# The row of mean squares in a two-mixer decoder layer: squares move under standing ones, and the row travels through DRAM ahead of its power

## The chip, the cores and the metric

The kernel runs on one core of one Trainium2 chip. The metric is the device time of one execution in microseconds (us), the median of several runs. One execution was also recorded by the profiler; its engines are TensorE (PE, with the weight loads as PEld), VectorE (DVE), ScalarE (ACT), GpSimd (POOL) and the queue of DMA issues on SyncE (SP). A second queue of DMA issues belongs to ScalarE.

## The reference

One layer on 1024 tokens of width 1024. The input is normed and modulated, one wide projection gives the parts, a gated spatial mixer gives `y_a`, and a state-space mixer (SSD) with 32 heads in 8 groups, in chunks of 128 tokens, gives `y_b`. What matters here is the step between the SSD mixer and its projection: an RMS norm over the 256 channels of each group, for each token.

```python
y_b = ssd_scan(xh, dt, a, bm, cm) + xh * d_skip[:, None]
yz = (y_b.reshape(b, s, SSM_D_INNER) * silu(ssm_z)).reshape(b, s, SSM_GROUPS, SSM_D_INNER // SSM_GROUPS)
y_b = rms_norm(yz, ssm_norm_w.reshape(SSM_GROUPS, -1)).reshape(b, s, SSM_D_INNER)
merged = sigmoid(g_a) * (y_a @ w_proj_a) + sigmoid(g_b) * (y_b @ w_proj_b)
return x + gate[:, None, :] * (merged @ w_out)
```
So for each group and token the kernel needs `(mean(yz*yz) + eps) ** -0.5`, a row of 1024 numbers per group.

## The kernel before

Channels lie on the 128 partitions and tokens along the free axis. Large products are made by a seven-product scheme on halves, in split precision. The order of the work is written out by hand for TensorE and for SyncE's loads: `mm`, `tp` and `load` (lines 80 to 90) are kept in program order. `store` (line 92) issues a DMA from ScalarE's queue and is placed by a scheduler, as are most operations of VectorE, ScalarE and GpSimd; those inside `tc.high_priority()` go first. The scheduler works with a simulated time of its own.

**The mixer phase** (about 932 to 1157 us) runs 32 steps, two groups taking turns, four steps of 256 tokens for each group. A step has three items, each a *slot*: `front` (the products inside the chunk `yi` and the new state `sp`), `back` (the product with the state `yn`, then `evacuate`) and `prep` for a later step (transposes and products into `pc` and `px`, then VectorE's products `dcy` on line 1027 and `xd`, `xe` on line 1023). Between the items TensorE is fed matmuls of the first projection (`pma`, drawn by `draw`). `later(n, f)` runs `f` n slots on. `fetch` loads the tiles `sl` and `dcy` of a step; there are five sets, so a load waits for the step five back to be done with its set.

**The row.** `evacuate` (line 1074) writes `yz`, the gated output, into a tile of 2 x 512 columns, of which there are four; the last operation is on GpSimd (line 1089). Eight steps later the same place is written again. After every second step `post` (line 1091) stores `yz` to `yb_d`, and
- 5 slots later `squares` (line 1106) squares it in place on ScalarE and adds the two halves on GpSimd (line 1109);
- 17 slots later `post2` (line 1111) sums the squares over the partitions: for each of four blocks of 128 tokens, the block of squares is the standing operand and a column of ones moves, which gives one column of `pq`. VectorE scales it into `ssq` (line 1117), tokens on partitions. When both halves of a group are there, GpSimd raises the 8 columns to the power −0.5 (line 1121);
- 8 slots after that `post3` (line 1125) transposes the 8 columns on TensorE into 8 rows of 128, VectorE copies them (line 1131) into a constant tile that is no longer used, and a store writes them to `rs_d`.

Groups 6 and 7 end last. Their second halves are squared into two tiles `sq` of their own, taken from two rings of two slots (line 1101), and summed in the next stage.

**The last stage** begins with the second projection: seven products `p1, p5, p2, p3, p6, p7, p4` of eight units each (`units`, line 1418). Unit `u` multiplies, then `ahead(u)` (line 1570) issues the loads of unit `u+6` and makes the operands of unit `u+4`. `y_load` (line 1406) loads a piece of `yb_d` (tile `yn`) and, for every second piece, the row of `rs_d` spread over the partitions (tile `rb`); `y_norm` (line 1414) multiplies them. The rows of groups 0 to 3 are wanted first, those of 6 and 7 from the loads of unit 20 on. `post2` of groups 6 and 7 stands behind units 1 and 4, `post3` behind units 4 and 6 (lines 1606 to 1613).

Of the kernel before, what the change touches and what calls it, by code (L numbers as in the profile page):

```python
# [12 lines left out]
ALU = mybir.AluOpType  # L13
# [3 lines left out]
P = 128  # L17
D = 1024
S = 1024
KT = D // P  # L20
NCH = S // P
NG = 8
# [3 lines left out]
EPS = 1e-6  # L26
# [9 lines left out]
def hybrid_kernel(  # L36
# [7 lines left out]
    V, A, G, PE = nc.vector, nc.scalar, nc.gpsimd, nc.tensor  # L44
# [8 lines left out]
    def dt_(shape, name):  # L53
        return dram.tile(shape, F32, name=name, tag=name)

    acs_d = dt_([NG, 4, HPG, 256], "acs_d")
    rs_d = [dt_([1, S], f"rs_d{g}") for g in range(NG)]
    v_d = dt_([NG, P, NCH * P], "v_d")
    ya_d = [dt_([P, S], f"ya_d{g}") for g in range(NG)]
    mt_d = [dt_([P, S], f"mt_d{g}") for g in range(NG)]  # L60
# [9 lines left out]
    def cst(shape, name, dt=F32):  # L70
        return const.tile(shape, dt, name=name, tag=name)
# [6 lines left out]
    pin = tc.keep_in_program_order  # L78

    def mm(acc, l, r, first=True, last=True):  # L80
        pin(PE.matmul(acc, l, r, start=first, stop=last))  # L81

    def tp(dst, src, idn):
        pin(PE.transpose(dst, src, idn))  # L84
# [4 lines left out]
    def load(dst, src):  # L89
        pin(nc.sync.dma_start(dst, src))  # L90

    def store(dst, src):
        nc.scalar.dma_start(dst, src)

    ident = cst([P, P], "ident")
    make_identity(nc, ident)
    ones = cst([P, P], "ones")
    G.memset(ones, 1.0)
    tri = cst([P, P], "tri")
    G.affine_select(out=tri, in_=ones, compare_op=ALU.is_ge, fill=0.0, base=0,  # L100
                    pattern=[[1, P]], channel_multiplier=-1)
    nhalf = cst([P, NCH], "nhalf")
# [13 lines left out]
    cwt = cst([P, P], "cwt")  # L116
# [9 lines left out]
    ssq = cst([P, NG * NCH + 24], "ssq")  # L126
# [365 lines left out]
    def later(delay, f, *a):  # L492
        tasks.append((slot[0] + delay, f, a))
# [478 lines left out]
    class Group:  # L972
# [118 lines left out]
        def post(self, q):  # L1091

            g = self.g
            for j in range(2):
                store(yb_d[2 * g + j][:, q * 512 : (q + 1) * 512], self.yz[q][:, j])
            yz = self.yz[q]
            if g < NG - 2 or q == 0:
                later(5, self.squares, yz, [yz[:, j] for j in range(2)])
                later(17, self.post2, q, [yz[:, 0]])
            else:  # L1100
                self.late = [turn(r, f"sq{g}", F32) for r in (y1_r, ym_r)]
                with tc.high_priority():
                    for j in range(2):
                        A.activation(self.late[j], yz[:, j], AF.Square)
# [4 lines left out]
            G.tensor_add(sq[0], sq[0], sq[1])  # L1109

        def post2(self, q, sq):
            g = self.g
            pq = rows_bank[0](f"pq{g}_{q}")
            for i in range(4):
                for j, t in enumerate(sq):
                    mm(pq[:, i : i + 1], t[:, i * P : (i + 1) * P], ones[:, 0:1], j == 0, j == len(sq) - 1)
            V.tensor_scalar(ssq[:, g * NCH + q * 4 : g * NCH + q * 4 + 4], pq[:, 0:4], 1.0 / 256, EPS,  # L1117
                            op0=ALU.mult, op1=ALU.add)
            if q == 1:
                c8 = slice(g * NCH, (g + 1) * NCH)  # L1120
                G.tensor_tensor(ssq[:, c8], ssq[:, c8], nhalf, op=ALU.pow)
                if g < NG - 2:
                    later(8, self.post3)

        def post3(self):

            g = self.g
            pr = rows_bank[0](f"pr{g}")
            tp(pr[0:NCH, 0:P], ssq[:, g * NCH : (g + 1) * NCH], ident)
            row = (cwt, tri)[g % 2][0:NCH, :]  # L1130
            V.tensor_copy(row, pr[0:NCH, 0:P])
            store(rs_d[g].rearrange("o (c p) -> (o c) p", p=P), row)

    groups = [Group(g) for g in range(NG)]
    rows_bank = [bank]
# [42 lines left out]
    def turn(r, name, dt=F32R):  # L1178
        tags, at = r
        at[0] += 1  # L1180
        return take(name, tags[(at[0] - 1) % len(tags)], dt)
# [187 lines left out]
    def banks(name, c):  # L1369
        return [psb.tile([P, 512], F32, name=f"{name}{j}", tag=f"b{c}{j}") for j in range(4)]  # L1370
# [12 lines left out]
    def slot_tile(name, dt=F32):  # L1383
        tag = room.pop(0)
        t = hp.tile([P, 512], dt, name=name, tag=tag)
        tags_of[name] = tag
        return t
# [82 lines left out]
    def multiply(u, ps):  # L1470
        nm, k = units[u]
        first = nm in ("p1", "p5", "p2", "p3")
        a, (bh, bl) = aops.pop(u), bops.pop(u)
        for j in range(4):
            js = slice(j * P, (j + 1) * P)
            for n, (v, r) in enumerate(((0, bh), (0, bl), (1, bh))):
                pin(PE.matmul(ps[j], a[:, v, js], r, start=first and n + k == 0, stop=n == 2 and k == KT - 1,  # L1477
                              skip_group_check=not first))
# [3 lines left out]
    def gate_load(b, h):  # L1482
        hs = slice(h * 512, (h + 1) * 512)
        th, ma = gate_slot(f"tg{b}_{h}"), gate_slot(f"ma{b}_{h}")
        load(th, th_d[(KT + b) * P : (KT + b + 1) * P, hs])
        load(ma, mt_d[b][:, hs])
        gates[b, h] = th, ma
# [82 lines left out]
    def ahead(u):  # L1570
        if u + LOAD < len(units):
            loads(u + LOAD)
        if u + LEAD < len(units):
            operands(u + LEAD)
# [15 lines left out]
    BESIDE = [(j // 2, wo_load, ("b11", j)) for j in range(4)] + [(2 + j, wo_load, ("t1", j)) for j in range(4)]  # L1590
    BESIDE += [(2 + j, wo_split, ("b11", j)) for j in range(4)]
    BESIDE += [(3 + j, row_load, (j,)) for j in range(5)] + [(j + 4, split, ("s1", j - 1)) for j in (1, 3)]
    for u, (nm, k) in enumerate(units):
        if k == 0:
            if nm == "p1":
                psy = banks("yp5", "y")
                psx = banks("x", "x")
                rows_bank[0] = lambda name: psy[("pr6", "pr7", "pq6_1", "pq7_1").index(name)]
            elif nm in ("p2", "p3"):
                psy = banks(f"y{nm}", "y")  # L1600
            elif nm == "p6":
                room.extend(rb_r[0])
            ps = psy if nm in ("p2", "p5", "p3") else psx
        multiply(u, ps)
        ahead(u)
        if nm == "p1" and k in (1, 4):
            late = groups[NG - 2 + k // 4]
            late.post2(1, late.late)
        if nm == "p1" and k == 4:
            for tags, _ in (y1_r, ym_r):  # L1610
                room.extend(tags)
        if nm == "p1" and k in (4, 6):
            groups[NG - 4 + k // 2].post3()
        if k % 2 and nm in GATES:
            gate_load(GATES[nm][0] + k // 2, GATES[nm][1])
        if nm == "p4":
            for at, f, a in BESIDE:
                if at == k:
                    f(*a)
        if k % 2 and more and nm not in ("p2", "p5"):  # L1620
            merged(*more.pop(0))
        if k == KT - 1:
            for j in range(4):
                with tc.high_priority():
                    if nm == "p1":
                        t = slot_tile(f"c11_{j}")
                        A.copy(t, psx[j])
                        more.append((j, 0, t, f"c11_{j}"))
                    elif nm == "p2":
                        V.tensor_add(more[j][2], more[j][2], psy[j])  # L1630
                    elif nm == "p5":
                        t = slot_tile(f"p5_{j}")
                        A.copy(t, psy[j])
                        sums.append(t)
                    elif nm == "p3":
                        t = slot_tile(f"p3_{j}")
                        V.tensor_add(t, sums[j], psy[j])
                        sums.append(t)
                    elif nm == "p6":
                        V.tensor_add(sums[4 + j], sums[4 + j], psx[j])  # L1640
                        more.append((j, 1, sums[4 + j], f"p3_{j}"))
                    elif nm == "p7":
                        V.tensor_add(sums[j], sums[j], psx[j])
                        more.append((4 + j, 1, sums[j], f"p5_{j}"))
                    elif nm == "p4":
                        merged(4 + j, 0, None, None)
# [166 lines left out]
```

## Time and profile before

| What | us or share |
|---|---|
| median of 3 runs | 1408.84 (1404.32 to 1409.13) |
| the profiled execution, own time | 1407.67 |
| its span in the profile | 1405.9 |
| granted TensorE clock | 0.997 |
| chain that ended last: TensorE, DMA, VectorE, GpSimd | 80%, 8%, 5%, 2% |
| DMA moved | 283.37 MB, mean 202 GB/s |

Start times in the rows are microseconds from the start of the span. A row of a timeline has the start, the time it takes, engine, line, operation, what is written from what, and how many were merged; in square brackets stands how long the engine was idle before it and what ended that. A row of the chain of work has a start, a length and what was at work. A row by tile has the shortest, middle and longest duration in nanoseconds, and the first and last start. Matmuls overlap in TensorE's pipeline, so the distance of two starts says more than a duration.

### The profile page before, as it was taken

The page shows a single profiled execution, that of the slowest core. Times are in us where ns is not written, and L with a number is a line of the kernel's source. Part 1 is how long each engine was busy: PE and PEld are TensorE (multiplying, and loading weights), DVE is VectorE, ACT ScalarE, POOL GpSimd, SP SyncE. Part 2 cuts the span into 40 slices and gives each one's busy share as a digit, 9 for nine tenths or more (in the row PEclk, how much of TensorE's full clock was granted, in tenths as well). Part 3 has the DMA queues.
Part 4 walks back from the last instruction along what each step waited for, and adds up shares of the span by engine and source line. Part 5 has one row for each costly group of instructions (what it writes and reads, how often), then busy time and mean ns, then how long its engine had stood idle before and what let it go on. Part 6 is the DMA issues. An engine that isn't in the chain of part 4 may idle for free.

```text
span 1405.9 us, 20633 instructions
## 1 busy us (share of the span) xinstructions
PE 1377.1 (98%) x7035; PEld 1139.9 (81%) x7035; DVE 1062.4 (76%) x1863; ACT 797.0 (57%) x1471; POOL 213.0 (15%) x208
## 2 busy tenths in 40 slices
PE   8999999999999999999999999999999999999997
PEld 6688888888888888888887888888888877878886
DVE  4786776777778889889788796388667767876976
ACT  5764576556656665556565555677766723322443
POOL 0000000000000011111000010038778740000001
PEclk9999999999999999999999999999999999999999
DMA  8653343343344777787675774598778749878903
GB/s 263 173 165 98 113 120 105 105 121 120 116 125 134 214 202 239 236 248 232 192 221 156 240 214 135 173 353 318 262 253 296 275 168 328 320 231 296 350 33 120
DMA packets 273150, 283.37 MB, mean 202 GB/s; under 512 B 15341, under 2 KB 223637, under 8 KB 273045
## 3 DMA queue, kind: packets, MB, share of 16 engines
q1 hardware_dynamic: 185684, 198.52, 44.4%
q10 hardware_dynamic: 87360, 83.54, 17.8%
q8 instruction: 55, 0.90, 0.3%
q14 instruction: 51, 0.41, 0.1%
HBM read 194.55 MB, written 87.46 MB: 201 GB/s over the span
## 4 chain that ended last, share of the span: by engine, by line
PE 80%; DMA 8%; DVE 5%; POOL 2%; issue 2%; ACT 1%; SPq 1%; ACTq 0%; DVEq 0%; POOLq 0%
PE xcb L574 6%; PE xuz L574 6%; PE xz L574 6%; PE xx L574 5%; PE xg L574 5%; PE x L1477 4%; PE yp L1477 4%; PE ox L1676 3%; PE yuz L574 3%; PE ycb L574 3%; PE pma L81 3%; PE xv L574 3%; PE yz L574 3%; PE yg L574 3%; PE yx L574 3%; DMA dcy<-acs_d 3%
## 5 line engine op out<-in xcount | busy, mean ns | idle before, releaser
L793 POOL TENSOR_TENSOR wog<-wog,gb 128x256 f32<-128x256 f32 x16 | 18.3, 1159 | 676.6 <-PE zz L574 413.3
L1007 ACT ACTIVATE dcy<-dcy,nacs 128x128 f32<-128x128 f32 x256 | 78.6, 388 | 14.9 <-POOL dcy L1002 14.5
L1002 POOL TENSOR_SCALAR_AFFINE_SELECT dcy<-dcy 128x1024 f32<-128x1024 f32 x32 | 35.0, 1095 | 135.7 <-ACT ea L999 132.3
L999 ACT ACTIVATE ea<-dcy 64x512 f32<-64x512 f32 x64 | 40.1, 626 | 14.2 <-DMA dcy<-acs_d 13.8
L920 ACT ACTIVATE ac<-ac 128x1024 f32<-128x1024 f32 x32 | 33.9, 1060 | 23.0 <-DVE ac L918 22.8
L81 PE MATMUL pma<-yh,wah 128*128 128x512 f32 x128 | 43.3, 419 | 0.0
L1027 DVE TENSOR_TENSOR dcy<-dcy,pc 128x1024 f32<-128x1024 f32 x32 | 39.0, 1218 | 4.8 <-PE pc L84 3.0
L81 PE MATMUL pma<-yh,wal 128*128 128x512 f32 x128 | 42.5, 413 | 0.0
L1089 POOL TENSOR_TENSOR yz<-y,sl 128x512 f32<-128x512 f32 x32 | 41.4, 1295 | 1.1
L1087 DVE TENSOR_TENSOR ym<-yn,ea 128x512 f32<-128x512 f32 (+1 forms) x32 | 19.9, 622 | 28.5 <-PE yn L81 28.3
L81 PE MATMUL pma<-yl,wah 128*128 128x512 f32 x128 | 40.1, 394 | 0.0
L1088 POOL TENSOR_TENSOR y<-y,ym 128x512 f32<-128x512 f32 (+1 forms) x32 | 36.6, 1144 | 14.4 <-DVE ym L1087 14.4
L81 PEld LDWEIGHTS yn<-sl,st 128*128 128x128 f32 x224 | 30.3, 190 | 8.3 <-issue 4.4
L81 PE MATMUL yn<-sl,st 128*128 128x128 f32 x224 | 31.6, 276 | 4.9 <-DVE st L1057 4.9
L1416 DVE SCALAR_TENSOR_TENSOR yn<-yn,par,rb 128x512 f32<-128x512 f32 x32 | 24.0, 749 | 15.7 <-DMA yn<-yb_d 15.5
L81 PE MATMUL sp<-xe,bn 128*128 128x256 f32 x112 | 32.6, 408 | 3.3 <-DVE ssq L1117 1.7
L81 PE MATMUL yi<-dcy,xd 128*64 128x128 f32 x512 | 35.7, 283 | 0.0
L918 DVE SCALAR_TENSOR_TENSOR ac<-c2x,cwt,ac 128x1023 f32<-128x1023 f32 (+2 forms) x24 | 31.2, 1300 | 5.3 <-ACT ac L916 5.1
L918 DVE SCALAR_TENSOR_TENSOR ac<-c2cb,cwt,ac 128x1023 f32<-128x1023 f32 (+2 forms) x24 | 31.1, 1296 | 4.4 <-ACT ac L916 4.3
L1691 POOL TENSOR_TENSOR r<-r,fnw 128x512 f32<-128x512 f32 x2 | 2.5, 1296 | 203.7 <-DMA out_dram<-r 203.7
L1055 POOL TENSOR_TENSOR st<-st,cd 128x256 f32<-128x256 f32 x48 | 32.1, 668 | 8.0 <-PE yn L81 5.3
L918 DVE SCALAR_TENSOR_TENSOR ac<-c1cb,cwt,ac 128x1023 f32<-128x1023 f32 (+2 forms) x24 | 31.6, 1318 | 1.3 <-ACT ac L916 1.3
(2980 smaller groups left out, 4390.9 us busy)
## 6 DMA issues: line engine op xcount, KB each, us to landing
sl<-s_d SPq DMA_DIRECT2D x32, 768.0 KB
s_d<-ac ACTq DMA_DIRECT2D x32, 512.0 KB
dcy<-acs_d SPq DMA_DIRECT2D x32, 512.0 KB
aw<-in_ada_w_dram SPq DMA_DIRECT2D x16, 512.0 KB
wbr<-in_w_proj_b_dram SPq DMA_DIRECT2D x64, 128.0 KB
wb_d<-wbb ACTq DMA_DIRECT2D x32, 256.0 KB
wb_d<-wbc ACTq DMA_DIRECT2D x32, 256.0 KB
yb_d<-yz ACTq DMA_DIRECT2D x32, 256.0 KB
```

The lines of the kernel that those rows point to most:

```text
L81: pin(PE.matmul(acc, l, r, start=first, stop=last))
L574: pin(PE.matmul(ps, lw[:, k * P : (k + 1) * P], r[k], start=first and n + k == 0, stop=n == 2 and k == 3, skip_group_check=not first))
L918: V.scalar_tensor_tensor(ac[:, s:], cc[:, : S - s], conv_wt[:, 3 - s, i : i + 1], ac[:, s:], op0=ALU.mult, op1=ALU.add)
L920: A.activation(ac, ac, AF.Silu)
L999: A.activation(ea[hh * HD : (hh + 1) * HD], dcy.rearrange("p (j e) i l -> p e j (i l)", e=2)[hh * HD : (hh + 1) * HD, hh], AF.Exp)
L1002: G.affine_select(out=d8, in_=d8, compare_op=ALU.is_ge, fill=-1e30, base=0, pattern=[[0, 2 * HPG], [1, P]], channel_multiplier=-1)
L1007: A.activation(dcy[:, h, i, :], dcy[:, h, i, :], AF.Exp, bias=sub[:, i, h : h + 1])
L1027: V.tensor_tensor(d3, d3, pc[:, 0:256].unsqueeze(1).to_broadcast([P, HPG, 256]), op=ALU.mult)
L1088: G.tensor_add(y1[:, :, t0:], y1[:, :, t0:], m[:, :, t0:])
L1089: G.tensor_mul(yz, y1, sl[:, 4:6])
L1477: pin(PE.matmul(ps[j], a[:, v, js], r, start=first and n + k == 0, stop=n == 2 and k == KT - 1, skip_group_check=not first))
L1676: pin(PE.matmul(ps, a[:, tsl], b[:, cs], start=first and n + j == 0, stop=n == 2 and j == 3, skip_group_check=not first))
```

## The change

`post2` comes 13 slots behind `post` instead of 17. The ones stand now (128 x 32) and a block of 128 squares moves; each of the four blocks goes into a strip of 32 partitions of one PSUM tile, every row of a strip holding the same sums. VectorE scales all 128 x 128 of it into the first 128 columns of the squares' own tile, and a store writes one row of each strip, four rows of 128, to a new DRAM row `ms_d`. `post3` is now a load from `ms_d` back into `ssq`, eight neighbouring tokens to a partition; `post4`, six slots on, is the power on GpSimd, now kept in program order; `post5`, three slots on, stores the result to `rs_d`. The transpose and its PSUM bank, the copy and the two constant tiles it was written to drop out. In the last stage the three steps stand behind units 3, 5 and 6 for group 6, and 7, 9 and 10 for group 7; `post2` stays behind units 1 and 4.

```diff
-                later(17, self.post2, q, [yz[:, 0]])
+                later(13, self.post2, q, [yz[:, 0]])
...
             pq = rows_bank[0](f"pq{g}_{q}")
-            for i in range(4):
-                for j, t in enumerate(sq):
-                    mm(pq[:, i : i + 1], t[:, i * P : (i + 1) * P], ones[:, 0:1], j == 0, j == len(sq) - 1)
-            V.tensor_scalar(ssq[:, g * NCH + q * 4 : g * NCH + q * 4 + 4], pq[:, 0:4], 1.0 / 256, EPS,
-                            op0=ALU.mult, op1=ALU.add)
-            if q == 1:
-                c8 = slice(g * NCH, (g + 1) * NCH)
-                G.tensor_tensor(ssq[:, c8], ssq[:, c8], nhalf, op=ALU.pow)
-                if g < NG - 2:
-                    later(8, self.post3)
+            for j, t in enumerate(sq):
+                for i in range(4):
+                    mm(pq[32 * i : 32 * i + 32, 0:P], ones[:, 0:32], t[:, i * P : (i + 1) * P], j == 0, j == len(sq) - 1)
+            row = sq[0][:, 0:P]
+            V.tensor_scalar(row, pq[:, 0:P], 1.0 / 256, EPS, op0=ALU.mult, op1=ALU.add)
+            store(ms_d[g][:, q * 512 : (q + 1) * 512].rearrange("o (i p) -> (o i) p", p=P), row[0:P:32, :])
+            if q == 1 and g < NG - 2:
+                for n, f in ((8, self.post3), (14, self.post4), (17, self.post5)):
+                    later(n, f)
 
         def post3(self):
 
-            g = self.g
-            pr = rows_bank[0](f"pr{g}")
-            tp(pr[0:NCH, 0:P], ssq[:, g * NCH : (g + 1) * NCH], ident)
-            row = (cwt, tri)[g % 2][0:NCH, :]
-            V.tensor_copy(row, pr[0:NCH, 0:P])
-            store(rs_d[g].rearrange("o (c p) -> (o c) p", p=P), row)
+            load(ssq[:, self.g * NCH : (self.g + 1) * NCH], ms_d[self.g].rearrange("o (p c) -> (o p) c", p=P))
+
+        def post4(self):
+
+            c8 = ssq[:, self.g * NCH : (self.g + 1) * NCH]
+            pin(G.tensor_tensor(c8, c8, nhalf, op=ALU.pow))
+
+        def post5(self):
+
+            store(rs_d[self.g].rearrange("o (p c) -> (o p) c", p=P), ssq[:, self.g * NCH : (self.g + 1) * NCH])
...
+    late_todo = {3: groups[NG - 2].post3, 5: groups[NG - 2].post4, 6: groups[NG - 2].post5,
+                 7: groups[NG - 1].post3, 9: groups[NG - 1].post4, 10: groups[NG - 1].post5}
...
-        if nm == "p1" and k in (4, 6):
-            groups[NG - 4 + k // 2].post3()
+        late_todo.get(u, lambda: None)()
```

More of the change, by code (lines that the diff above doesn't have):

```diff
@@ L57, in hybrid_kernel @@
     rs_d = [dt_([1, S], f"rs_d{g}") for g in range(NG)]
+    ms_d = [dt_([1, S], f"ms_d{g}") for g in range(NG)]
     v_d = dt_([NG, P, NCH * P], "v_d")
@@ L1597, in hybrid_kernel @@
                 psx = banks("x", "x")
-                rows_bank[0] = lambda name: psy[("pr6", "pr7", "pq6_1", "pq7_1").index(name)]
+                rows_bank[0] = lambda name: psy[1 + ("pq6_1", "pq7_1").index(name)]
             elif nm in ("p2", "p3"):
```

## Prediction

> **What bounds the kernel now.** I read the page's first part, then the busy time by stretches of the mixer phase, then the chain of work.
>
> ```profile
> PE 1377.1 (98%) x7035; PEld 1139.9 (81%) x7035; DVE 1062.4 (76%) x1863; ACT 797.0 (57%) x1471; POOL 213.0 (15%) x208
> ```
> ```profile
> 940.00:980.00 40.00, 39.95 (x300) 34.24 (x299) 33.77 (x57) 27.20 (x73) 30.87 (x31) 1.00 0.90 310
> 1100.00:1130.00 30.00, 27.75 (x207) 24.20 (x208) 21.65 (x42) 18.88 (x49) 23.49 (x25) 1.00 0.64 219
> 1160.00:1200.00 40.00, 37.77 (x183) 31.50 (x184) 30.99 (x51) 16.03 (x29) 3.29 (x2) 1.00 0.93 336
> ```
> Over the span TensorE is busy 98%, so a microsecond of TensorE work counts nearly everywhere. The stretches (columns: TensorE, weight load, VectorE, ScalarE, GpSimd, clock, DMA share) say that the phase of the change is less simple: at 940 DMA is 0.90 busy and GpSimd 31 of 40 us, at 1100 GpSimd has 23.5 of 30, and at 1160 DMA is at 0.93. The chain shows what ends last in each:
>
> ```profile
> 960.66 6.55 DMA dcy<-acs_d
> 988.51 1.05 PE pq L81 x8
> 1040.04 0.79 PE pq L81 x8
> 1046.30 0.79 PE pq L81 x8
> 1065.33 0.79 PE pq L81 x8
> 1072.06 0.79 PE pq L81 x8
> 1122.14 1.60 POOL ssq L1121
> 1131.06 1.64 POOL ssq L1121
> 1133.31 2.27 DMA yn<-yb_d
> 1145.70 0.79 PE pq L81 x8
> 1181.51 1.66 POOL ssq L1121
> ```
> The chain changes owner: loads of dcy, then TensorE from about 1030 to 1079, then GpSimd to 1133, then loads of the last stage. So of 14 sums of squares (tile pq) only six stand on the chain, and of the eight powers (ssq, L1121) three. What is taken from the others buys idle time.
>
> **TensorE, part by part.** A sum has four matmuls, each recorded twice: squares standing, one column of ones moving. After, 32 columns of ones stand and 128 columns of squares move, into four strips of 32 partitions. The nearest rows in four strips are the matvec's (tile pm, first rows), with 256 moving columns:
>
> ```profile
> 981.06 0.95 PE L81 MATMUL pq<-ones,yz 128*128 128x1 f32 x8
> 981.94 1.09 PE L81 MATMUL yi<-dcy,xd 128*64 128x128 f32 x16
> 14.95 1.07 PE L81 MATMUL pm<-aw,scz 128*32 128x256 f32 x16
> ```
> ```profile
> 23.90 0.58 PEld L81 LDWEIGHTS pm<-aw,scz 128*32 128x32 f32 x15
> ```
> Before: 981.94 − 981.06 = 0.88 us for 8 records. After, from below: 15 loads of 32 columns in 0.58 us, 0.039 each, so 8 take 0.31. From above: 1.07/16 = 0.067 with twice the columns, so 0.54; if strips did not overlap at all, 0.88 as now. I take 0.40, near the lower end, because half the columns move; it saves **0.48 per sum**. The Trainium skill, TensorEngine Tiling (Array Packing), section Tiling Modes, speaks against it: changing the mode (not just the tile) drains TensorE, and here the array goes to four strips and back 16 times. It gives no figure; by an estimate from the two pm rows, a drain of 1.07 − 0.58 = 0.49 us would eat the saving. This hangs on that page: by that rule the third rival below results, and the trace is not against it, though the 1.07 holds its own mode changes.
>
> On the chain, six sums give 6 × 0.48 = **−2.9**. The transposes of post3 go, 0.11 each:
>
> ```profile
> 1138.78 0.11 PE pr L84
> ```
> Four of six in the phase lie in TensorE stretches: **−0.4**.
>
> **VectorE and ScalarE.** The eviction grows from 128x4 to 128x128; the copies of 8x128 go.
>
> ```profile
> L1117 DVE TENSOR_SCALAR ssq<-pq x14: 150/152/163, 983.4 to 1150.4; 128x4 f32<-128x4 f32 x14
> L1131 DVE COPY cwt<-pr x3: 269/269/269, 1031.8 to 1139.4; 8x128 f32<-8x128 f32 x3
> ```
> The copy also reads 128 columns from PSUM, so I take 0.27: 16 × 0.12 = 1.9 more, 8 × 0.27 = 2.2 less, nothing in sum. The place matters more. With 13 slots instead of 17 (three slots a step: front, back, prep) the sum falls between back and prep, not between prep and front. It pushes prep's pc matmuls back by 0.40 and the eviction pushes the product dcy (L1027) by up to 0.27; where VectorE's chain through prep leads, that is lost. I count four of the 14 such, and the 0.40 alone, since the eviction is at least not longer than the copies that went: 4 × 0.40 = **+1.6**; bounds 0 and 14 × 0.67 = 9.4.
> ScalarE issues 16 stores to ms_d more and 8 to rs_d as before, at 0.3 us in its sequencer. A store waiting for VectorE holds what stands behind it on ScalarE:
>
> ```profile
> 1181.98 1.14 ACT L1455 CAST p5bh<-yn 128x512 fp32r<-128x512 f32 x2 [6.60 <-DVE cwt L1131]
> ```
> That is the store of rs_d today: the cast behind it came 6.60 late. In the mixer phase I cost the new stores at nothing, since ScalarE is 27 of 40 us busy; without that cover it is 16 × 0.3 = 4.8.
>
> **GpSimd.** The pow keeps its 1.65 us but goes 14 slots behind the sums. For groups 4 and 5 that is behind the last step, when GpSimd is done: the two on the chain (1122, 1131) leave it. Those of groups 2 and 3 come in, at about 1091 and 1098, where GpSimd has gaps. From 0 to −3.2; I take one pow, **−1.6**. The mixer phase sums to −2.9 − 0.4 + 1.6 − 1.6 = **−3.3**.
>
> **Waits that tighten.** Sums need the squares' add on GpSimd; and the tile yz is now held until the ms_d store has landed.
>
> ```profile
> L1089 POOL TENSOR_TENSOR yz<-y,sl x32: 1271/1286/1608, 941.7 to 1146.0; 128x512 f32<-128x512 f32 x32
> 992.27 1.29 POOL L1109 TENSOR_TENSOR yz<-yz 128x512 f32<-128x512 f32 x1
> 1008.91 0.95 PE L81 MATMUL pq<-ones,yz 128*128 128x1 f32 x8
> 1046.14 0.95 PE L81 MATMUL pq<-ones,yz 128*128 128x1 f32 x8
> 1053.67 1.27 POOL L1089 TENSOR_TENSOR yz<-y,sl 128x512 f32<-128x512 f32 x1
> 1014.94 1.12 ACTq L93 DMA_DIRECT2D yb_d<-yz  x2
> 1022.37 0.63 ACT L1108 ACTIVATE yz<-yz 128x512 f32<-128x512 f32 x1 [2.95 <-DMA yb_d<-yz]
> ```
> A step is (1146.0 − 941.7)/31 = 6.6 us, so four slots are 8.8. The closest add ends at 993.56, 15.35 before its sum: 6.5 stay. The closest reuse comes 7.5 behind its sum (1053.67 − 1046.14); 16.3 stay for eviction, issue and a landing. Stores on this queue land in up to 1022.37 − 1014.94 = 7.4. Both hold, at no cost. Without the cover, a store landing later would delay yz, then the DMA issue behind it on SyncE that waits for yz's engine.
>
> **The last stage.** The sums of groups 6 and 7 (16 records each) and their transposes stand among the products:
>
> ```profile
> 1164.07 1.84 PE L81 MATMUL yp<-ones,sq 128*128 128x1 f32 x16
> 1165.77 0.49 PE L1477 MATMUL x<-p1bh,p1a 128*128 128x512 f32 x1
> 1183.21 0.27 PE L84 MATMUL yp<-ident,ssq 128*8 128x128 f32 x1 [1.69 <-POOL ssq L1121]
> ```
> Each sum goes from 1.70 to 0.80: −1.8. Two transposes: −0.2. TensorE's 1.69 of waiting for group 7's power goes, for no TensorE work needs it any more: −1.7. Together **−3.7**. What is late next is the operands of p5. In their way stands the new load of ms_d on SyncE's pinned queue: at unit 7 it stands behind p5's loads for k=5 and ahead of all others, and holds them until the store has landed.
>
> ```profile
> 1178.65 0.32 SPq L90 DMA_DIRECT2D rb<-rs_d  x1
> ```
> ```profile
> 1181.27 0.15 DVE L1117 TENSOR_SCALAR ssq<-yp 128x4 f32<-128x4 f32 x1
> 1186.56 0.75 DVE L1416 SCALAR_TENSOR_TENSOR yn<-yn,par,rb 128x512 f32<-128x512 f32 x1 [0.55 <-DMA yn<-yb_d]
> 1187.23 0.68 DVE L1456 TENSOR_TENSOR p5bl<-yn,p5bh 128x512 fp32r<-128x512 f32 x1
> ```
> ```profile
> 1186.09 0.39 PE L1477 MATMUL yp<-p5bh,p5a 128*128 128x512 f32 x1
> 1207.85 0.39 PE L1477 MATMUL yp<-p2bh,p2a 128*128 128x512 f32 x1
> ```
> The load at 1178.65 (k=6) is the first held. The eviction of group 7 ran only at 1181.27, behind VectorE's waits, though its matmuls were done at 1175.8. So the store issues at about 1181.9 and lands in 2.3 (the quickest landing above, yn at 1133.31) to 7.4 us: 1184.2 to 1189.3. Hold: 5.5 to 10.6. Behind it on VectorE: the norm of k=6 (1186.56) stands ahead of p5's low part for k=3 (1187.23, done 1187.9). TensorE takes (1207.85 − 1186.09)/8 = 2.72 a unit, so it wants k=3 at 1194.25 today and, 3.7 earlier, at 1190.5: 2.6 us of hold are free. At the short end 5.5 − 2.6 = 2.9 come back as a wait. I take that end, since the store is 2 KB where the 7.4 is of two stores of 256 KB; DMA at 0.93 speaks against it. Stage: −3.7 + 2.9 = **−0.8**; bounds −3.7 (no hold that counts) and −3.7 + 8.0 = +4.3. Group 6's load holds SyncE at 1169 likewise, and group 7's squares reuse the ring slot of group 6's, so they wait for that landing too; ScalarE's casts queue behind them.
>
> The Trainium skill, DMA: Bandwidth & Descriptors, section Anatomy of one DMA, gives a fixed cost of about 2.0 us, mostly the write's receipt. By it the hold would be 5.2 or 5.3 and the stage about −1.1. Three transfers in a row would be 6.0 by that page, an estimate; the 2.27 row agrees with the size of one.
>
> **Sum.** −3.3 − 0.8 = −4.1 against the profiled execution's own 1407.67 (span 1405.9, 1.77 around it that the change doesn't touch): 1403.57, so **1403.5**. That execution is 1.2 under the median 1408.84, and inside the runs' 1404.32 to 1409.13.
>
> **Rivals.**
> 1. *Everything counts* (chance 0.18): TensorE is the bound throughout. For it: 98% busy. Against it: only six of 14 sums on the chain. 14 × 0.48 + 6 × 0.11 = 7.4, two pows 3.2, stage 3.7: −14.3, **1393.4**.
> 2. *SyncE held too long* (0.24), the other side. Place: the ms_d loads of groups 6 and 7 in the pinned queue. Price: holds of up to 5.4 (1169.3 to a landing at 1174.7) and 10.6, 16.0 in all; DMA at 0.93 cannot make them up. From 2.6 + 3.7 + 3.3 = 9.6 us of hold on, the kernel is slower than before. At 16.0 that is +6.4, **1414**; with the mixer phase's gain absent as well 1417.4. For it: eviction behind VectorE's waits, DMA full. Against it: loads run six units, 16 us, ahead.
> 3. *It does not do what it says, or is hidden* (0.10): strips that do not overlap, or a drain each time, and the phase paced by DMA and GpSimd. Then the 2.9 and 1.8 go, and prep waits 0.88 in four steps: −0.4 + 3.5 − 1.6 = +1.5 for the phase; −0.2 − 1.7 = −1.9 for the stage, with 2.6 + 1.8 = 4.4 of hold free and 5.5 − 4.4 = 1.1 given back. In all +0.7, **1408.4**.
>
> **How the numbers follow.** The forecast has 0.48, its own range 1399.5 to 1407. A measurement of this kernel tells about 0.5% (7 us) from no change, so faster means under 1401.8 and slower over 1415.9. Faster: rival 1's 0.18 and the lower part of the forecast, 0.18: 0.36. Slower: three quarters of rival 2, its range pushed by group 6's squares waiting as well: 0.18. Same: 0.46. The range runs from rival 1's 1393 to 1415, inside rival 2; it leaves out about 0.2, mostly above.
>
> **What would show it.** Right: pq as eight records in about 0.40 us; no matmul reading ssq and no wait of TensorE for GpSimd near 1180; powers of groups 4 and 5 behind the last yz; a pause in SyncE's queue before the ms_d loads, and a wait of TensorE within p5's first four units. Wrong: pq at 0.8; waits of yz (L1089) for a store, or of a pow for a load; casts waiting for stores throughout the mixer phase. A changed order on VectorE around units 4 to 8 would move the stage's term most.

## The result, and the profile after

The changed kernel takes **1412.3 us** (median of 16 runs, 1409.04 to 1417.78), the kernel before 1407.86 in the same rounds (16 runs, 1404.32 to 1415.04): a ratio of **1.0037**, 95% interval 1.0026 to 1.0049. It is slower by 0.37%, where 0.3% faster was forecast. The profiled execution after took 1411.77 (span 1410.0, granted clock 0.994).

The first part of the page, then the busy time by stretches, of the kernel after:

```profile
PE 1375.2 (98%) x7027; PEld 1129.5 (80%) x7027; DVE 1060.5 (75%) x1855; ACT 792.0 (56%) x1471; POOL 212.9 (15%) x208
```
```profile
940.00:980.00 40.00, 39.95 (x307) 34.12 (x305) 32.83 (x56) 28.00 (x75) 32.07 (x32) 1.00 0.92 302
1100.00:1130.00 30.00, 28.41 (x220) 23.68 (x217) 23.86 (x44) 22.46 (x61) 25.07 (x27) 1.00 0.73 250
1160.00:1200.00 40.00, 35.30 (x171) 28.13 (x170) 26.85 (x44) 12.79 (x24) 3.73 (x2) 0.91 0.81 282
```
The page hides it: TensorE has 1.9 us less to do and is still 98% busy. The last row shows it: in those 40 us TensorE lost 2.5 us of work, the DMA engines fell from 0.93 to 0.81, and the granted clock from 1.00 to 0.91. That is the stage in which groups 6 and 7 get their rows.

The operations did what the change says. Grouped by line, in the mixer phase, before and after; then, after, a sum in the chain of work, the eviction of `pq` and GpSimd's timeline:

```profile
L81 PE MATMUL pq<-ones,yz 128*128 128x1 f32 x96 | 11.6, 242 | 0.5 <-DVE st L1057 0.4
```
```profile
L82 PE MATMUL pq<-yz,ones 128*32 128x128 f32 x104 | 5.5, 285 | 0.1
```
```profile
1144.15 0.36 PE pq L82 x8
```
```profile
L1120 DVE TENSOR_SCALAR yz<-pq x14: 279/281/284, 977.6 to 1145.1; 128x128 f32<-128x128 f32 x14
```
```profile
1145.47 1.29 POOL L1090 TENSOR_TENSOR yz<-y,sl 128x512 f32<-128x512 f32 x1
1146.72 3.25 POOL L1133 TENSOR_TENSOR ssq<-ssq,nhalf 128x8 f32<-128x8 f32 x2
```
By busy time a sum (8 records) fell from 11.6/12 = 0.97 us to 5.5/13 = 0.42; by the distance of starts, in which the prediction reckons, it fell from 0.88 to 0.36. So the strips do overlap; the eviction takes 0.28; the powers of groups 4 and 5 run behind the last `yz`.

The chain of work in the last stage of the kernel after (start, length, what was at work; pieces left out marked):

```profile
1169.84 0.77 DVE yn L1421
...
1171.32 0.21 DVE sq L1120
...
1171.56 2.72 DMA ms_d<-sq
1174.30 0.32 SPq L91
...
1175.14 5.02 DMA yn<-yb_d
...
1180.26 0.76 DVE yn L1421
...
1183.69 0.29 DVE sq L1120
...
1184.00 2.99 DMA ms_d<-sq
1187.01 0.32 SPq L91
...
1189.37 6.59 DMA p5a<-wb_d
```
This is a loop that is run through twice. A norm on VectorE, the eviction behind it, the store to `ms_d`, SyncE's held load, the `yn` load behind that, the norm that waits for it, the next eviction. SyncE's queue and the engines show the same from their side:

```profile
1168.68 0.37 SPq L91 DMA_DIRECT2D p5a<-wb_d  x1
1174.30 0.32 SPq L91 DMA_DIRECT2D ssq<-ms_d  x1
...
1181.67 0.32 SPq L91 DMA_DIRECT2D p5a<-wb_d  x1
1187.01 0.32 SPq L91 DMA_DIRECT2D ssq<-ms_d  x1
```
```profile
1174.30 0.63 ACT L1105 ACTIVATE sq<-yz 128x512 f32<-128x512 f32 x1 [7.84 <-DMA ms_d<-sq]
```
```profile
1174.99 1.08 PE L82 MATMUL yp<-sq,ones 128*32 128x128 f32 x16 [4.70 <-ACT sq L1105]
...
1210.68 0.60 PE L1482 MATMUL yp<-p2bh,p2a 128*128 128x512 f32 x1 [2.51 <-ACT p L1639]
```
Two holds of SyncE, from the end of one issue to the next, 1174.30 − 1169.05 = 5.25 and 1187.01 − 1181.99 = 5.02 us, 10.3 in all; ScalarE's second square of group 7 waits for the landing of group 6's store; TensorE waits 4.70 for the square and 2.51 at the start of `p2`.

One table for what follows, in us, worked out from the starts of TensorE's first and last instruction of each kind in each trace: the *mixer* from the first `yi` to the last `yn`, the *stage* from the first product of `p1` to the first of `p3`, and from there to the span's end.

| profiled kernel | mixer | stage | rest |
|---|---|---|---|
| before | 218.0 | 73.5 | 175.5 |
| after | 214.7 | 79.3 | 175.7 |
| e1_late_old | 215.2 | 76.3 | 176.0 |
| e2_late_only | 215.3 | 77.3 | 175.9 |
| e3_own_tile | 216.3 | 78.1 | 175.5 |
| e5_both | 216.6 | 76.5 | 175.5 |
| f1_pool_load | 215.4 | 75.9 | 175.3 |
| f2_fill | 211.9 | 82.5 | 175.5 |
| f3_pool_stores | 209.8 | 72.3 | 176.2 |
| f4_idle_stores | 218.0 | 72.8 | 175.3 |
| g1_all_pool | 209.3 | 73.8 | 176.7 |
| g2_before_pool | 215.8 | 73.4 | 177.6 |
| g3_pool_ms | 215.6 | 76.6 | 175.8 |
| h1_fill_less | 216.6 | 81.2 | 175.7 |

Two parts are left out: what lies ahead of the first `yi` (924.4 to 932.0 us; 2.8 more in the kernel after than before), and what lies between the mixer and the stage (13.3 to 13.5 us where groups 6 and 7 are as before, about 12.0 where they go the new way). With them the two profiles' difference adds up: 2.8 − 3.3 − 1.4 + 5.8 + 0.2 = 4.1 us.

Each is one execution: `before`, `e2`, `f1`, `f4` and `g2` have the same mixer but for the queue of a few stores, and lie between 215.3 and 218.0. The new way with its stores on ScalarE lies between 211.9 and 216.6, and there the time goes with the granted clock of the mixer: 211.9 at 1.00 (`f2`), 214.7 at 0.99 (`after`), 215.2 to 216.6 at 0.98 (`e1`, `e3`, `e5`, `h1`). So a mixer of 214.7 against 218.0 shows nothing, and that the difference is 3.3, the number of the forecast, is chance; a mixer below 210 does show something.

### The profile page after: what moved, and what is told of

It reads as the page before. It is cut to its first block, busy times and chain, and to the rows that moved or that the text cites. A ratio compares the mean times of both kernels' runs of the same rounds, so it can differ in the third digit from the quotient of the medians.

```text
span 1410.0 us, 20648 instructions
## 1 busy us (share of the span) xinstructions
PE 1375.2 (98%) x7027; PEld 1129.5 (80%) x7027; DVE 1060.5 (75%) x1855; ACT 792.0 (56%) x1471; POOL 212.9 (15%) x208
## 4 chain that ended last, share of the span: by engine, by line
PE 72%; DMA 11%; DVE 7%; ACT 3%; issue 3%; POOL 2%; SPq 1%; ACTq 0%; DVEq 0%; POOLq 0%
PE xuz L575 6%; PE xcb L575 6%; PE xx L575 5%; PE xz L575 5%; PE xg L575 5%; PE x L1482 4%; PE ox L1682 3%; PE yuz L575 3%; PE xv L575 3%; PE ycb L575 3%; PE pma L82 3%; PE yx L575 3%; PE yg L575 2%; DMA yn<-yb_d 2%; PE oy L1682 2%
## 5 line engine op out<-in xcount | busy, mean ns | idle before, releaser
L82 PEld LDWEIGHTS yi<-dcy,xd 128*64 128x64 f32 x512 | 28.0, 139 | 6.0 <-issue 3.2
```

## The experiments

Theory A at first: the mixer phase gains as forecast, and the last stage loses more than it. Its rival B: the last stage is as it was, and the mixer phase loses. The ratios are those to the kernel before in the same rounds.

**e1_late_old**: groups 0 to 5 in the new way, 6 and 7 wholly as before (`post2o` is the `post2` of before, with its transposes and banks).

```diff
-                later(13, self.post2, q, [yz[:, 0]])
+                later(13 if g < NG - 2 else 17, self.post2 if g < NG - 2 else self.post2o, q, [yz[:, 0]])
```


> Groups 0 to 5 in the new way, groups 6 and 7 wholly in the old way (ones moving, transpose behind units 4 and 6). Theory A, the loss sits in the last stage: between the two profiles the mixer phase (first yz to first product of p1) went from 215.2 to 210.6 us, the stage from p1's first product to p3's first from 73.5 to 79.3. Undoing the stage's part keeps the 4.6 and loses the 5.8: about 1403, ratio 0.997 to before. Theory B, the loss is made by groups 0 to 5 (or by the 2.75 us that the changed kernel was behind before the mixer phase began): the ratio stays at about 1.003.

Measured: 1410.27, ratio 1.0020 (1.0004 to 1.0036), between the two answers and nearer B's.

**e2_late_only**: the reverse, groups 0 to 5 as before, 6 and 7 in the new way.

> Groups 0 to 5 in the old way, groups 6 and 7 in the new. Theory A: all of the stage's loss and none of the phase's gain, about 1413, ratio 1.004. Theory B: no change, ratio within 0.999 to 1.001.

Measured: 1413.71, ratio 1.0041 (1.0027 to 1.0055). Neither theory holds alone. The last stage loses with the late groups, as A says; but groups 0 to 5 have no gain, and by the interval they lose a little, as B says. In e1's profile that loss does not stand in the mixer (215.2, before 218.0) but in the stage (76.3, before 73.5). Both halves had to be explained. (0.20% and 0.41% do not add up to the 0.37% of both; the intervals just allow it.)

**e3_own_tile**: the changed kernel, with the late rows evicted into constant tiles that are no longer used, so that group 7's squares needn't wait for group 6's store.

```diff
-            row = sq[0][:, 0:P]
+            row = sq[0][:, 0:P] if len(sq) == 1 else (cwt, tri)[g % 2]
```


> The changed kernel, but the rows of groups 6 and 7's second halves go to a constant tile that is no longer used, so that group 7's squares no longer wait for the landing of group 6's store. SyncE's holds stay. Theory A1, the ring slot is the price: TensorE's 4.7 us of waiting for group 7's squares goes and most of it is kept, about 1408, ratio 1.000. Theory A2, SyncE's holds (5.2 and 3.3 us waited for ms_d) are the price: the operands of p5 stay late, TensorE waits at p5's or p2's start instead, 1411 to 1412, ratio 1.003.

Measured: 1412.64, ratio 1.0046 (1.0027 to 1.0065). TensorE's wait of 4.70 for the square is gone from the profile, and the time is not: TensorE waits 2.24 in `p5` and 4.61 at the start of `p2` instead. The wait was a place where lost time showed, not its cause.

**e5_both**: e3, and the loads of `ms_d`, powers and stores of groups 6 and 7 two units later.

```diff
-    late_todo = {3: groups[NG - 2].post3, 5: groups[NG - 2].post4, 6: groups[NG - 2].post5,
-                 7: groups[NG - 1].post3, 9: groups[NG - 1].post4, 10: groups[NG - 1].post5}
+    late_todo = {5: groups[NG - 2].post3, 7: groups[NG - 2].post4, 8: groups[NG - 2].post5,
+                 9: groups[NG - 1].post3, 11: groups[NG - 1].post4, 12: groups[NG - 1].post5}
```


> As e3, and the ms_d load, the power and the store to rs_d of groups 6 and 7 stand two units later (5, 7, 8 and 9, 11, 12), so that SyncE reaches the loads after the stores have landed. Theory A: both waits gone, the stage at its predicted -3.7 against before and the phase at -4.6, so 1400 to 1403, ratio 0.995 to 0.997. If only the ring slot mattered, the same as e3. Theory B: 1410 or more.

Measured: 1411.52, ratio 1.0028 (1.0011 to 1.0045). Less than hoped. SyncE is still held, from 1173.03 to 1177.61 and from 1185.81 to 1187.38, 6.2 us in place of 10.3, and the stage takes 76.5. Later is better, but the loads still stand in the queue that everything else stands in.

**f1_pool_load**: e2 with e3's tile, and the two late loads of `ms_d` on GpSimd's queue (`G`), which has nothing else to do there.

```diff
-            load(ssq[:, self.g * NCH : (self.g + 1) * NCH], ms_d[self.g].rearrange("o (p c) -> (o p) c", p=P))
+            pin(G.dma_start(ssq[:, self.g * NCH : (self.g + 1) * NCH], ms_d[self.g].rearrange("o (p c) -> (o p) c", p=P)))
```


> Groups 0 to 5 as before; groups 6 and 7 in the new way, with a row of their own, and their two loads of ms_d issued from GpSimd's queue, which has nothing else to do in this stage, in place of SyncE's. Theory A (the last stage loses because SyncE, which issues the weights' loads in order, is held behind the two loads of ms_d): the last weight load of p2 is issued 54 to 56 us after the last yn (61.9 in the kernel with only groups 6 and 7 in the new way), p1's start to p3's start takes 73.5 to 74.5 us (77.3), ratio 0.999 to 1.001. Rival B (the way over DRAM is too long or stops TensorE wherever the load is queued): 77 us and a ratio of 1.003 to 1.005 as with SyncE.

Measured: 1408.46, ratio 1.0014 (0.9997 to 1.0032), against e2's 1.0041. SyncE's row of the last weight of `p2`, after and here:

```profile
1204.93 0.33 SPq L91 DMA_DIRECT2D p2r<-in_w_proj_b_dram  x1
```
```profile
1198.90 0.38 SPq L91 DMA_DIRECT2D p2r<-in_w_proj_b_dram  x1
```
Counted from the last `yn` that is 61.9 us after, 58.3 here, and 54.5 before. So SyncE's hold is a cause, as the theory says, but not the whole: by time two thirds of e2's loss go with it (0.41% to 0.14%, with wide intervals), by the stage in one profile a third (77.3 to 75.9, where 74.5 at most was expected). The trace has a candidate for the rest: SyncE now waits 4.2 us for the landing of the late stores to `rs_d`, which the loads of `rb` must follow (0.3 us before).

**f2_fill** and **h1_fill_less**: the changed kernel with 32 and 22 matmuls that nothing reads, where TensorE waited 4.70. The clock was the suspect: it falls after such a pause.

```diff
+            if k == 4:
+                for _ in range(32):
+                    mm(psy[3][:, 0:P], ident, ones)
             late = groups[NG - 2 + k // 4]
```


> The changed kernel with 32 matmuls of ident by ones into an unused bank ahead of group 7's sum, where TensorE waited 4.70 us; they add work that nothing reads. Theory C (the pause also costs the clock that is granted after it): the wait there falls to about 1.2 us, the rows from 1174 to 1180 show 1.00 in place of 0.50, and the time falls by about 1.7 us (half of 3.4 us), ratio 1.002 to 1.003. Rival D (the stage waits for loads, so that TensorE's speed in these us does not matter): the clock is mended and the later waits grow by as much, ratio 1.0035 to 1.0045 as in the changed kernel.

> The changed kernel with 22 matmuls of ident by ones, which nothing reads, ahead of group 7's sum. With 32 of them the filling took 7.30 us (two records of 0.114 us each), longer than the pause of 4.70 and the product ahead of it, and so put off the sum itself; 22 take 5.0 and should end before the squares are there. Theory C (the granted clock of 0.50 after the pause costs time): rows at 1.00 from 1174 to 1180, sum no later than 1175.0, ratio 1.002 to 1.003 against the kernel before. Rival D (the stage waits for loads, so that the clock in these us does not matter): clock mended, ratio 1.0035 to 1.0045 as in the changed kernel, and the time shows up again as waits for operands in p5 or at p2's start.

Measured: f2 1414.64, ratio 1.0059 (1.0039 to 1.0079); h1 1416.29, ratio 1.0072 (1.0053 to 1.0092). In f2 the filling was twice as long as meant (7.30 us), since each matmul is two records. In h1 it took 5.07 and held the clock; the stretches, SyncE and TensorE of h1:

```profile
1170.00:1175.00 5.00, 5.00 (x41) 4.77 (x40) 2.31 (x5) 0.00 (x0) 0.00 (x0) 1.00 0.93 301
1175.00:1180.00 5.00, 5.00 (x43) 4.13 (x42) 2.68 (x4) 2.16 (x4) 1.85 (x1) 1.00 0.47 116
```
```profile
1191.51 0.32 SPq L91 DMA_DIRECT2D ssq<-ms_d  x1
```
```profile
1189.94 0.80 PE L1482 MATMUL yp<-p5bh,p5a 128*128 128x512 f32 x1 [3.21 <-DVE sq L1120]
```
The clock is 1.00 where it was 0.50, and the kernel is slower. The second load of `ms_d` goes out 46.7 us after the last `yn` (1144.8), against 44.0 in the kernel after: the loop of the chain turned later, and the stage took 81.2. Counted from the last `yn`, TensorE reached `p5` 2.9 us sooner than in the kernel after (40.4 against 43.3), and then waited 3.21 for an operand; behind that wait the clock stood at 0.50 from 1190 to 1196. So the gain of theory C does not show: what the filling won was waited away within the first unit of `p5`, as rival D has it. But the ratio is neither C's nor D's. That h1 is slower than the kernel after by more than the delay of its loop stays unexplained, and that SyncE alone sets the time here is argued, not shown.

**f3_pool_stores**: e1 with the 18 stores of `ms_d` and `rs_d` of groups 0 to 5 on GpSimd's queue in place of ScalarE's.

```diff
-            store(ms_d[g][...], row[0:P:32, :])
+            (G.dma_start if g < NG - 2 else store)(ms_d[g][...], row[0:P:32, :])
...
-            store(rs_d[self.g][...], ssq[...])
+            (G.dma_start if self.g < NG - 2 else store)(rs_d[self.g][...], ssq[...])
```


> Groups 0 to 5 in the new way, 6 and 7 as before, and the stores of ms_d and rs_d of groups 0 to 5 issued from GpSimd's queue in place of ScalarE's. Theory A (the mixer phase of the new way loses because ScalarE, in order, is held by these stores, which wait for VectorE's eviction, GpSimd's power and the landing of earlier transfers, and the copies of bn behind them come late): no wait of TensorE for bn over 2 us, ratio 0.999 to 1.001 in place of 1.002. Rival B (18 issues cost GpSimd as much): ratio 1.002 to 1.006, with waits for GpSimd's st and dcy. Rival C (the mixer phase is no slower, and the 1.002 lies elsewhere): 1.002 without waits for bn.

Measured: **1400.71, ratio 0.9959 (0.9944 to 0.9974)**, where the same stores on ScalarE gave 1.0020: 0.6%, or 8.6 us, hang on this one edit to 18 small stores, more than theory A asked. First the stretch 970 to 1050, before, in e1 and in f3:

```profile
970.00:1050.00 80.00, 74.64 (x569) 65.26 (x566) 56.81 (x106) 56.50 (x152) 60.20 (x59) 0.98 0.79 272
```
```profile
970.00:1050.00 80.00, 74.85 (x592) 62.43 (x594) 59.90 (x108) 55.46 (x148) 62.50 (x60) 1.00 0.84 287
```
```profile
970.00:1050.00 80.00, 78.48 (x628) 65.96 (x628) 64.46 (x114) 57.02 (x152) 69.48 (x72) 1.00 0.80 278
```
TensorE stood idle for 80 − 74.64 = 5.4 us before, for 5.2 in e1 and for 1.5 in f3. (The kernel after has 3.5 here, and a wait of 3.59 for `bn` just behind, up to 1053.16.) Over the whole mixer it is 8.7, 8.5 and 5.1: with the stores on ScalarE the waits are as long as before, in f3 they are shorter. Two places in e1 show a hold. ScalarE and TensorE near 1048, then ScalarE and GpSimd at the end of the phase, all of e1:

```profile
1043.66 0.33 ACTq L1338 DMA_DIRECT2D mt_d<-tha  x1
1046.16 0.34 ACTq L94 DMA_DIRECT2D rs_d<-ssq  x1
1046.55 0.63 ACT L1109 ACTIVATE yz<-yz 128x512 f32<-128x512 f32 x1 [4.27 <-DVE ym L1088]
```
```profile
1048.79 0.44 PE L85 MATMUL px<-ident,sl 128*128 128x128 f32 x2 [2.70 <-ACT bn L1030]
```
```profile
1144.75 3.25 POOL L1133 TENSOR_TENSOR ssq<-ssq,nhalf 128x8 f32<-128x8 f32 x2
```
```profile
1147.14 3.37 ACTq L94 DMA_DIRECT2D rs_d<-ssq  x2
1150.55 0.62 ACT L1483 CAST p1bh<-yn 128x512 fp32r<-128x512 f32 x1 [9.49 <-DMA yb_d<-yz]
```
Between 1043.99 and 1046.16 ScalarE issues nothing and computes nothing; the copy of `bn` stands behind, and TensorE waits for it. The chain of work of e1 says what ended the hold:

```profile
1038.44 7.65 DMA sl<-s_d
...
1046.16 0.34 ACTq L94
```
It was not the power, which ended at 1041.18, but the landing at 1046.09 of a load sent at 1038.44. In the kernel after the same store goes out at 1050.55, likewise just behind the landing of a load of `sl` (sent at 1041.17, landed at 1050.47), and the wait of 3.59 for `bn` follows. Why a store to `rs_d` waits for that load the traces do not say. At the end the stores of groups 4 and 5 stand behind the two powers, which stand behind the last `yz`, and `p1`'s first cast stands behind the stores: it starts at 1150.55, 9.5 us after the last `yn` (1141.0). The second power ended at 1148.00, the issue of the second store 2.5 us later. In f3 it starts 2.7 us after (last `yn` 1137.6):

```profile
1140.27 0.62 ACT L1483 CAST p1bh<-yn 128x512 fp32r<-128x512 f32 x1 [2.54 <-DVE tha L1336]
```
The stage is 72.3 in f3 and 76.3 in e1, with groups 6 and 7 treated alike in both. The late cast does not put off `p1`, whose first product comes 13.4 us after the last `yn` in both kernels. The difference shows later in `p1`: TensorE waits for group 7's power (0.94 in f3), and behind the wait it runs at half the clock. TensorE's row and the stretch behind it, in e1:

```profile
1181.67 0.38 PE L85 MATMUL yp<-ident,ssq 128*8 128x128 f32 x1 [4.39 <-POOL ssq L1149]
```
```profile
1181.00:1186.00 5.00, 4.33 (x11) 3.47 (x12) 4.30 (x8) 1.28 (x4) 0.61 (x1) 0.50 1.04 400
```
How the late cast leads there is not shown.

The edit also changes more than the queue. With the stores moved, the scheduler places the operations of GpSimd, ScalarE and VectorE in the mixer in another order. GpSimd near 990, in e1 and in f3:

```profile
989.58 0.73 POOL L1089 TENSOR_TENSOR y<-y,ym 128x256 f32<-128x256 f32 x1
990.28 1.29 POOL L1110 TENSOR_TENSOR yz<-yz 128x512 f32<-128x512 f32 x1
```
```profile
989.54 0.72 POOL L1089 TENSOR_TENSOR y<-y,ym 128x256 f32<-128x256 f32 x1
990.22 0.61 POOL L1056 TENSOR_TENSOR st<-st,cd 128x256 f32<-128x256 f32 x1
990.95 1.28 POOL L1110 TENSOR_TENSOR yz<-yz 128x512 f32<-128x512 f32 x1
```
No run has the new order with the stores on ScalarE. So the 8.6 us belong to the queue together with the order that it brings; that they are the holds' alone is not shown.

**f4_idle_stores**: the kernel before with 12 stores more on ScalarE's queue, of ones, which nothing reads.

```diff
+            if g < NG - 2:
+                store(ms_d[g][:, q * 512 : (q + 1) * 512].rearrange("o (i p) -> (o i) p", p=P), ones[0:P:32, :])
```


> The kernel before with 12 more stores of 4x128 on ScalarE's queue, from the standing ones into ms_d, at the places of the groups' sums; nothing reads them, and they wait for no engine, only for what every transfer waits for. Theory A1 (a store on ScalarE costs by itself, since it waits for the landing of an earlier transfer): ratio 1.001 to 1.003 and longer waits for bn. Rival A2 (only the wait for the eviction and the power costs): ratio 0.9995 to 1.0005.

Measured: 1407.41, ratio 1.0008 (0.9992 to 1.0024). The interval holds zero and part of what A1 asks: stores that wait for no engine cost little or nothing in the kernel before, where they leave the order of the other operations as it was. It does not tell the two apart.

**g1_all_pool**: the changed kernel with all stores of `ms_d` and `rs_d`, and the two late loads, on GpSimd's queue, with e3's tile; the edits are those of f1 and f3 for all groups.

> The changed kernel with every store of ms_d and rs_d on GpSimd's queue, the two late loads of ms_d there too, and a row of their own for the late groups. If both readings hold (the mixer phase loses by the stores on ScalarE's queue, the last stage by the two loads on SyncE's), both parts are mended at once: ratio 0.994 to 0.997, mixer (first yi to last yn) about 210 us, p1's start to p3's start at most 74 us. Rival (the new way in the last stage costs something wherever its transfers are queued): 0.998 to 1.001, with p1 to p3 at 76 us or more.

Measured: **1401.1, ratio 0.9956 (0.9940 to 0.9972)**. Both halves are mended together: mixer 209.3, stage 73.8. It beats the kernel before as f3 does, and the two can't be told apart.

**g2_before_pool**: the kernel before with its six stores of `rs_d` of groups 0 to 5 on GpSimd's queue.

> The kernel before, with the six stores of rs_d of groups 0 to 5 issued from GpSimd's queue in place of ScalarE's: the change of queue without the change. Theory A (the new way of summing gains in the mixer once its stores hold nobody): here 0.998 to 1.001, so that the 0.996 of the run with all stores of these groups on GpSimd is the new way's. Rival Q (the gain is the queue's alone, and the new way has none): 0.995 to 0.997 here as well.

Measured: 1407.07, ratio 1.0001 (0.9988 to 1.0013). In the kernel before the queue is worth nothing; rival Q falls. The gain of f3 and g1 belongs to the new way of summing with its stores on GpSimd's queue, and the order of work that comes with them.

**g3_pool_ms**: f3, but the six stores of `rs_d` stay on ScalarE.

> Groups 0 to 5 in the new way, 6 and 7 as before; only the twelve stores of ms_d on GpSimd's queue, the six of rs_d on ScalarE's. If the stores of rs_d, which stand behind GpSimd's power and an earlier transfer's landing, hold the copies of bn: ratio 1.000 to 1.002, with waits of TensorE for bn as with all stores on ScalarE. If the stores of ms_d hold them, by their number and by VectorE's eviction: 0.995 to 0.997 as with all of them moved.

Measured: 1404.97, ratio 0.9991 (0.9976 to 1.0006), between both answers: by the middle values each kind of store carries about half, 0.3%, though the interval touches e1's and f3's. Its stage is e1's (76.6), as it should be if the stores of groups 4 and 5 to `rs_d` are what lengthens it. (Its profiled execution, 1409.2, is one of the slower ones.)

## Why the prediction was wrong, point by point

- **TensorE.** Right. 0.40 for a sum was forecast, 0.36 came, and the fear of a drain that eats the saving did not come true: the rival that goes with what the Trainium skill (TensorEngine Tiling (Array Packing), section Tiling Modes) states, that a change of mode drains TensorE, had a sum at 0.88. The rows of `pq` leave room for a small drain at most.
- **Eviction, transposes, powers.** Right: 0.28 for 0.27, no transpose left, the powers of groups 4 and 5 off the phase.
- **"In the mixer phase I cost the new stores at nothing, since ScalarE is 27 of 40 us busy."** This step failed. A share of idle time is no cover for a queue that runs in order: in e1 a store that waited stopped the copies and casts behind it from 1043.99 to 1046.16 and again behind the last `yz`, busy or not. The prediction said so of the cast at 1181.98 one sentence earlier, and names casts that wait for stores as a sign of being wrong, but did not carry it into the sum; its price "without that cover", 4.8, counted only 0.3 us of issue each. Between e1 and f3 it is 8.6 us, with the order that changes along. So groups 0 to 5, forecast at −3.3, cost +2.8 (e1's 0.20%) where −5.8 (f3's 0.41%) was to be had.
- **What may have been counted too low.** Once the waits are gone, −5.8 is near twice the forecast −3.3, on the way to rival 1, *everything counts*. Whether more than "six of fourteen" sums count, or the waits alone are shorter, is not shown apart.
- **"Behind it on VectorE ... 2.6 us of hold are free."** This failed too. The sizes were right: 5.4 was given for group 6's hold and 5.25 came, 5.5 at the short end for group 7's, and 5.02 came. The two stores landed 2.72 and 2.99 us after their issue, nearer to 2.3 than to 7.4; the figure of about 2.0 us that the prediction takes from the Trainium skill (DMA: Bandwidth & Descriptors, section Anatomy of one DMA) is given there for DMAs issued from GpSimd, and these went out from ScalarE. But the hold was set against TensorE's wish for one operand, six units of lead away. The chain shows that the two holds stand in series, since group 7's eviction waits on VectorE for a norm whose `yn` stands behind group 6's load. The lead was eaten by the first hold. The stage grew by 79.3 − 73.5 = 5.8 where −0.8 was forecast. By the profiles 3.8 of it come with the late groups (e2, 77.3), and 2.8 come with groups 0 to 5 alone (e1, 76.3). f1 says that SyncE's holds are part of it; with all stores off ScalarE as well (g1, 73.8) nearly all is gone, though g1 moves the late stores and those of groups 0 to 5 at once.
- **The power's wait of 1.69 goes.** It did, and TensorE waited 4.70 and 2.51 elsewhere in the stage. That group 7's squares wait for group 6's landing was foreseen; in e3 nothing is won without it.
- **Rivals.** Rival 2, SyncE held too long, names the right place for the last stage; its own rule turns the sign from 9.6 us of hold on, and the holds are 10.3. By that rule the kernel would be 0.7 us slower; 4.4 came. It was given a chance of 0.24 and should have had more, since the loop over VectorE could be read from the order of the code. Rival 3 falls by the 0.36. No rival had the mixer's stores.

What stays open: how much of the 8.6 us is the holds of ScalarE's queue and how much the new order of work; why a store to `rs_d` waits for the landing of an earlier load (near 1046 it did, in e1, and not for the power; f4's interval is too wide to price that by itself). And what the 0.14% left in f1 is, if it is anything: the interval reaches below zero.

## What to carry to other kernels

An added DMA is priced by the queue that it is put on: list what stands behind it in that queue, and what it waits for, and give no credit for the engine's idle share. A load that must follow a store, put into the queue that feeds the whole stage, can close a loop with that stage's own operands; then each hold delays the next, and no lead covers it. Before judging a change of the arithmetic, try its small transfers on a queue where nobody waits: here the same sums gave +0.37% with their transfers on ScalarE's and SyncE's queues and −0.44% with all but the early loads on GpSimd's. Then look whether the scheduler has kept the order of the rest.

## What the runs showed of the hardware

TensorE's granted clock can fall to one half behind a pause, and the length of the pause alone does not decide it. Kernel f2 has two pauses of nearly the same length 25 us apart. TensorE's row and the stretch behind it, first the one, then the other; last the kernel after, behind its wait of 4.70:

```profile
1187.43 0.50 PE L1482 MATMUL yp<-p5bh,p5a 128*128 128x512 f32 x1 [2.06 <-DVE sq L1120]
```
```profile
1188.00:1190.00 2.00, 2.00 (x6) 1.61 (x5) 0.69 (x1) 0.57 (x1) 0.00 (x0) 0.51 0.02 2
```
```profile
1212.36 0.50 PE L1482 MATMUL yp<-p2bh,p2a 128*128 128x512 f32 x1 [2.12 <-ACT p L1642]
```
```profile
1212.00:1214.00 2.00, 1.64 (x7) 1.38 (x8) 1.92 (x4) 2.00 (x5) 0.00 (x0) 1.00 0.92 252
```
```profile
1174.00:1176.00 2.00, 1.01 (x17) 0.60 (x17) 0.74 (x2) 1.66 (x3) 0.00 (x0) 0.50 0.11 10
```
Behind 2.06 us the clock was 0.51, behind 2.12 us it was 1.00. In f4 a pause of 1.49 us (up to 1133.56) was followed by 0.50, and one of 3.14 us (up to 1035.97) by 1.00. The Trainium skill, TensorE: Matmul & The Clock Gate, section Part 1: The HAM clock gate, has the half rate after at least one idle window of about 3.4 us, in windows that run freely; here 1.49 us was enough once, and 3.14 us was not. In h1 the clock kept up bought nothing, since TensorE then waited for an operand. In e1 it does cost: behind the wait of 4.39 TensorE runs without another wait to the end of `p5`, at 0.50 for some 4.5 us, about 2 us by an estimate from these rows.

The 18 small stores did better from GpSimd's queue than from ScalarE's (SyncE's was not tried), though the Trainium skill, DMA: Bandwidth & Descriptors, section Issuing engine by pattern, gives simple stores to SyncE and calls the hardware queues generally faster. In this kernel what counted was who stood behind them, and in what order the rest was placed.
